# Where the weight splits of the first block stand in ScalarE's queue

## The chip, the cores and the metric

The kernel runs on one core of one Trainium2 chip. The metric is the device time of one execution in microseconds (us). Engines are called as in the profile: PE is TensorE (matmuls), ACT is ScalarE, DVE is VectorE, POOL is GpSimd, SP is SyncE, which here only issues transfers (DMA).

## The reference

One step of a hybrid recurrent decoder: 2048 prompt tokens and 64 sample tokens (8 sequences of 8), 1024 channels. What is computed, shortened:

```python
u = rms_norm(x, norm_pre)
z = u @ w_in        # lru_x, lru_gate, q|k|v, gdn_gate, b, a, two merge gates
lru_xc = conv4(lru_x) + lru_conv_b
h = rg_lru(lru_xc, ...)              # gates by 8 blocks of 128, then a scan over time
lru_out = h * silu(lru_gate)
qkv = silu(conv4(gdn_qkv))           # 8 heads of 128
gdn_out = norm(gated_delta_rule(l2norm(q), l2norm(k), v, g, beta)) * silu(gdn_gate)
merged = sigmoid(m_lru) * (lru_out @ w_br_lru) + sigmoid(m_gdn) * (gdn_out @ w_br_gdn)
y = x + rms_norm(merged @ w_out, norm_post)
```

All is in float32. States of the convolutions, of the LRU and of the delta rule are outputs too.

## The kernel before

**Precision.** A float32 product is made of three matmuls of rounded parts: every operand is held as a high part and the rest. For weights, `split` writes `hi` (ScalarE, a rounding copy) and then `lo` = source - `hi` (GpSimd; VectorE for `w_out`). A projection accumulates hi x high (L551), hi x rest (L553) and lo x high (L555) for each of eight k steps, so the third matmul of a projection is the first that needs `lo`. In the trace both parts of a weight have the name `whl`; the raw weight is `raw`, `raws` or `rawo` (128 x 1024).

**Blocks.** The prompt is done in four blocks of 512 tokens. The first block also takes the 64 sample tokens (576 columns, in halves of 256 and 320). In the first block each of 88 weight tiles is loaded, split, used, and stored to a scratch place in DRAM (`dW`, by SP); the later blocks read it back prepared. A ring of three `whl` buffers holds the split weights, so a split waits until the store of the buffer's last content has ended.

**Order of the first block.** First `u` is normalised and transposed: `u_norm` and eight `u_tile`s, each with ScalarE writing the high part `a` of 512 and of 64 columns and VectorE the rest (L358). A small projection with 16 columns of `w_in` (for beta and the decay; its weights are cast from `wraw` to `wst3`) follows. Then the *K stage*: for heads 0 to 7 the projection K (evacuated by ScalarE into `cvr`, `cvy`, `cvs`, then the convolution on VectorE, L582 for the prompt and L588 for the samples, then `th`, a tanh on ScalarE) and a merge-gate projection M (evacuated into `tmo`, which is stored as `dtm`). Then the *LRU stage*: eight groups X of 128 channels, with M8 to M14 between them; the convolved group is split into `xh` and `xl`, the block gates' weights `gwr` into `gwh` and `gwl`, and the gate matmuls (`g`) are evacuated by ScalarE into `lt`. Then the *Q stage*: per head Q, V and the head's gate, with the delta rule of the heads woven in, then the two branch projections, and `w_out` in four column groups of two weights each (evacuated with `yj`).

**What sets the order.** TensorE's order is the order of the program text. On the other engines a scheduler orders instructions by their priority, as dependences allow. `wfetch` is what brings weights: it issues the load of a raw weight, the store of an older split one, and the split. In the first block `proj` takes the next weight and calls `wfetch(1)`, so the split of weight n+1 stands in the text at the start of projection n. `A`, which stands for ScalarE, is a wrapper: when `A.after` is set, each later ScalarE instruction of the text gets an edge (of order, without a semaphore) behind that instruction:

```python
            if self.after is not None:
                self._tc.add_manual_dep(r.ins, self.after.ins.name, ..., reason="weights first")
```

`proj` sets `A.after` to the newest split. The scheduler can thus place a split early, ahead of older ScalarE work, and nothing younger may pass it.

Of the kernel before, what the change touches and what calls it, by code (L numbers as in the profile page):

```python
# [154 lines left out]
def body(ctx, tc, x_prompt, x_sample, state_lru_conv, state_lru_h, state_gdn_conv, state_gdn_S,  # L155
# [5 lines left out]
    V, T, SP = nc.vector, nc.tensor, nc.sync  # L161
    A, G = Ordered(tc, nc.scalar), nc.gpsimd
# [32 lines left out]
    def tr(out, in_, idn):  # L195
        T.transpose(out, in_, idn)  # L196
        W.pe(TR)
# [5 lines left out]
    def split(hi, lo, src, eng=None):  # L203
        r = A.activation(hi, src, AF.Copy)
        (eng or G).tensor_tensor(out=lo, in0=src, in1=hi.bitcast(F32), op=OP.subtract)  # L205
        return r
# [28 lines left out]
    key = lambda e: (e[0].tensor.name, e[1])  # L235
# [4 lines left out]
    wstores, wraws = [], {}  # L240

    wready = []
    wlast = [None]
    wnext, lnext = [0], [0]
    ring, wx = [0], []

    def wtile():
        ring[0] += 1
        if wx and ring[0] % 4 == 0:
            return wx[0].tile([128, 2, 1024], F32R, name="whx", tag="whx")  # L250
        return wp.tile([128, 2, 1024], F32R, name="whl", tag="whl", bufs=3)

    def wload(n):

        src, c = e = worder[n]
        if key(e) in wraws:
            return
        if isinstance(c, tuple):
            raw = rw.tile([128, 4, 256], F32, name="rawo", tag="raws")
            SP.dma_start(raw, src[c[1] * 512:(c[1] + 1) * 512, c[0] * 256:(c[0] + 1) * 256]  # L260
                         .rearrange("(k p) c -> p k c", p=128))
            wraws[key(e)] = raw
        elif not (paired[0] <= n < paired[1] or paired[2] <= n < paired[3]):
            raw = rw.tile([128, 8, 128], F32, name="raws", tag="raws")
            SP.dma_start(raw, src[:, c:c + 128].rearrange("(k p) c -> p k c", p=128))
            wraws[key(e)] = raw
        else:
            two = [key(x) for x in worder[n:n + 7]].count((src.tensor.name, c + 128))
            w = 128 + 128 * two
            raw = rp[0].tile([128, 8, w], F32, name="raw", tag="raw")  # L270
            SP.dma_start(raw, src[:, c:c + w].rearrange("(k p) c -> p k c", p=128))
            for j in range(1 + two):
                wraws[src.tensor.name, c + 128 * j] = raw[:, :, 128 * j:128 * j + 128]

    def wstore(held=0):

        while len(wstores) > held:
            i, hl = wstores.pop(0)
            SP.dma_start(dW[i], hl.bitcast(F32))

    def wfetch(ahead):

        while wnext[0] < len(worder) and len(wready) < ahead:
            n = wnext[0]
            e = worder[n]
            place = wplace[key(e)]
            out = isinstance(e[1], tuple)
            hl = wtile()
            hi, lo = (hl[:, j].rearrange("p (k c) -> p k c", c=256 if out else 128) for j in range(2))
            if n < len(wplace):  # L290
                while lnext[0] < len(wplace) and lnext[0] <= n + (
                        2 if paired[0] <= lnext[0] < paired[1] else 1):
                    wload(lnext[0])
                    lnext[0] += 1
                wstore(1)
                wlast[0] = split(hi, lo, wraws[key(e)], V if out else None)
                wstores.append((place, hl))
            else:
                wstore()
                SP.dma_start(hl.bitcast(F32), dW[place])  # L300
            wready.append((hi, lo))
            wnext[0] += 1
# [21 lines left out]
    def u_load(bn, pool):  # L324
        nt = NCH + (1 if bn == SB else 0)
        xh = []
        for i in range(nt):
            m = 128 if i < NCH else NS
            xt = pool.tile([128, D], F32, name=f"ux{i}")
            SP.dma_start(xt[:m], xp[bn * TB + i * 128: bn * TB + (i + 1) * 128] if i < NCH else xs)  # L330
            xh.append((xt, m))
        return xh
# [44 lines left out]
    wst3 = wst[:, 0:256].rearrange("p (k c) -> p k c", c=32)  # L377
# [34 lines left out]
    with tc.tile_pool(name="init", bufs=2, side="right") as ip:  # L412
        with tc.tile_pool(name="u0", bufs=1) as up:
            r0 = ip.tile([8, 128], F32, name="r0")
            SP.dma_start(r0, rows(norm_pre))
            xh = u_load(0, up)
            t = gtile()
            tr(t[:, :8], r0, ident[:8, :8])
            V.tensor_copy(npre, t[:, :8])
            wraw = ip.tile([128, 8, 16], F32, name="wraw", bufs=1)  # L420
            SP.dma_start(wraw, win[:, C_B:C_B + 16].rearrange("(k p) c -> p k c", p=128))
            u_norm(xh, up)
            for n in range(2):
                wload(n)
                lnext[0] += 1
            SP.dma_start(dtb, bass.AP(tensor=gdn_dt_bias.tensor, offset=gdn_dt_bias.offset, ap=[[0, 128], [1, 8]]))
            SP.dma_start(negA, bass.AP(tensor=gdn_A_log.tensor, offset=gdn_A_log.offset, ap=[[0, 128], [1, 8]]))
            u = [u_tile(xh, k) for k in range(8)]
            zz = ip.tile([128, 96], F32, name="zz", bufs=1)
            V.memset(zz, 0.0)  # L430
            V.tensor_copy(wst[:, 256:352], zz)
            V.tensor_copy(wst3[:, :, 0:16], wraw)
            V.tensor_tensor(out=wst3[:, :, 16:32], in0=wraw, in1=wst3[:, :, 0:16].bitcast(F32), op=OP.subtract)
            wfetch(2)
        G.affine_select(out=tri, in_=ones, pattern=[[1, 128]], compare_op=OP.is_ge, fill=0.0,
                        base=0, channel_multiplier=-1)
        G.affine_select(out=offm.rearrange("p (a b) -> p a b", b=32), in_=ones.rearrange("p (a b) -> p a b", b=32),
                        pattern=[[-32, 4], [0, 32]], compare_op=OP.is_ge, fill=0.0, base=-32,
                        channel_multiplier=1)
        V.tensor_scalar(offm, offm, -1.0, None, op0=OP.mult)  # L440

        blk = const.tile([64, 64], F32, name="blk")
        blk3 = blk.rearrange("p (a b) -> p a b", b=8)
        G.affine_select(out=blk3, in_=ones[:64, :64].rearrange("p (a b) -> p a b", b=8),
                        pattern=[[-8, 8], [0, 8]], compare_op=OP.is_ge, fill=0.0, base=0, channel_multiplier=1)
        G.affine_select(out=blk3, in_=blk3, pattern=[[8, 8], [0, 8]], compare_op=OP.is_ge, fill=0.0,
                        base=7, channel_multiplier=-1)
        tris = const.tile([64, 64], F32, name="tris")
        V.tensor_tensor(out=tris, in0=blk, in1=tri[:64, :64], op=OP.mult)
        negs = const.tile([64, 64], F32, name="negs")  # L450
        V.tensor_scalar(negs, tris, 1.0, BIG, op0=OP.subtract, op1=OP.mult)
        bsel = blk3[:, :, 0]
        G.memset(halog, 0.0)
        G.memset(halol, 0.0)
        G.memset(hlast, 0.0)
        tc.keep_in_program_order(A.activation(negA, negA, AF.Exp))
        V.tensor_scalar(negA, negA, -1.0, None, op0=OP.mult)
# [73 lines left out]
    for blkno in range(NBLK):  # L531
# [9 lines left out]
        def proj(mov, evac):  # L541
            w = nextw()
            wfetch(3 if blkno else 1)
            A.after = wlast[0]
            hi, lo = w
            for c0, n in halves:
                ps = pmm.tile([128, 512], F32, name="mm", tag="mm")
                for k in range(8):
                    mh, ml = mov[k]
                    wh = hi[:, k, :]  # L550
                    T.matmul(ps[:, :n], wh, mh[:, c0:c0 + n], start=k == 0, stop=False)  # L551
                    W.pump(n * 0.4219)
                    T.matmul(ps[:, :n], wh, ml[:, c0:c0 + n], start=False, stop=False)  # L553
                    W.pump(n * 0.4219)
                    T.matmul(ps[:, :n], lo[:, k, :], mh[:, c0:c0 + n], start=False, stop=k == 7)  # L555
                    if k < 7:
                        W.pump(n * 0.4219)
                evac(ps, c0, n)
                W.pump(n * 0.4219)
# [654 lines left out]
        for k in range(8):  # L1214
            hi = pA.tile([128, TB + NS], F32R, name="a", tag="a")
            lo = pA.tile([128, TB + NS], F32R, name="a", tag="a")
# [20 lines left out]
        for dd in range(8):  # L1237
# [5 lines left out]
            hi = Bp.tile([128, NB], F32R, name="bt", tag="bt")  # L1243
            lo = Bp.tile([128, NB], F32R, name="bt", tag="bt")
# [108 lines left out]
```

## Time and profile before

| | |
|---|---|
| time, median of 3 runs | 2684.38 us (2678.17 to 2687.7) |
| profiled execution, its own time | 2683.59 us |
| its span | 2681.9 us |
| mean granted TensorE clock | 0.987 |
| PE busy | 2571.7 us (96%) |
| DVE, ACT, POOL busy | 1503.4, 885.4, 565.8 us (56%, 33%, 21%) |

The span is the time from the first to the last instruction of the profiled execution; a share is of the span. A row of the timeline has the start, the duration, engine, line, operation, and the tiles with the shape; in brackets is the engine's idle time before the instruction and what released it. L143 is the line in the wrapper at which each ScalarE instruction is made, so ScalarE's work is told apart by its tiles. The first block ends at about 868 us of the span.

### The profile page before, as it was taken

Reading aid. Unit: us, or ns where it says so; the run is one execution under the profiler, and the core shown is the slowest. Engines: PE = TensorE matmul, PEld = TensorE weight load, DVE = VectorE, ACT = ScalarE, POOL = GpSimd, SP = SyncE. Lnnn points to the kernel's source line nnn. Section 1 sums busy time; section 2 is a strip of 40 time slices with the busy share of each in tenths; the row PEclk is TensorE's granted clock in tenths of the full one; section 3 lists DMA queues with packets and bytes.
Section 4 is the critical chain, followed back from the end, with each engine's and each line's share of the span. In section 5 each row is a group of like instructions: output and inputs, shape, how many; then the busy total and the mean of one; then the engine's idle time right before and its main releaser. Section 6 shows DMA issues by size and latency. Waiting matters only on the chain.

```text
span 2681.9 us, 39950 instructions
## 1 busy us (share of the span) xinstructions
PE 2571.7 (96%) x15332; PEld 2237.5 (83%) x15332; DVE 1503.4 (56%) x3441; ACT 885.4 (33%) x1722; POOL 565.8 (21%) x444
## 2 busy tenths in 40 slices
PE   6888799999999999999999999999999999999999
PEld 5887798888999788888889888888889888888888
DVE  4668477787434557566522557566513458566512
ACT  5324543333324225333302235333303235333301
POOL 2442342232540211100120121110210211110200
PEclk9988899999999999999999999999999999999999
DMA  7987978789887887554466787544466887555465
GB/s 190 250 257 187 228 207 187 203 176 179 255 292 256 283 277 222 200 177 158 154 237 256 260 283 225 203 163 163 154 245 256 270 272 217 200 172 168 160 236 200
DMA packets 327897, 581.82 MB, mean 217 GB/s; under 512 B 70849, under 2 KB 236762, under 8 KB 282650
## 3 DMA queue, kind: packets, MB, share of 16 engines
q1 hardware_dynamic: 313882, 553.57, 66.9%
q10 hardware_dynamic: 13824, 25.70, 2.5%
q8 instruction: 121, 1.98, 0.3%
q14 instruction: 70, 0.57, 0.1%
HBM read 421.61 MB, written 157.59 MB: 216 GB/s over the span
## 4 chain that ended last, share of the span: by engine, by line
PE 68%; DMA 3%; issue 2%; DVE 1%; POOL 1%; ACT 1%; SPq 0%; ACTq 0%; POOLq 0%; DVEq 0%
PE mm L555 17%; PE mm L551 16%; PE mm L553 16%; PE g L192 5%; PE c L192 4%; PE mm L1294 2%; PE mm L1298 2%; PE mm L1296 2%; PE g L196 2%; DMA er<-dgc 1%; DMA dgc<-gr 0%; DMA npb<-in_norm_post_dram 0%; DMA ux<-in_x_prompt_dram 0%; DMA whl<-dW 0%; POOL er L756 0%
## 5 line engine op out<-in xcount | busy, mean ns | idle before, releaser
L551 PE MATMUL mm<-a,whl 128*128 128x512 f32 (+2 forms) x2432 | 865.0, 356 | 25.2 <-ACT tmo L143 18.5
L555 PE MATMUL mm<-a,whl 128*128 128x512 f32 (+2 forms) x2432 | 869.6, 358 | 4.8 <-POOL whl L205 4.8
L553 PE MATMUL mm<-a,whl 128*128 128x512 f32 (+2 forms) x2432 | 863.9, 355 | 0.0
L551 PEld LDWEIGHTS mm<-a,whl 128*128 128x128 f32 x2432 | 466.7, 192 | 74.7 <-ACT tmo L143 20.0
L555 PEld LDWEIGHTS mm<-a,whl 128*128 128x128 f32 x2432 | 466.7, 192 | 58.0 <-POOL whl L205 5.4
L553 PEld LDWEIGHTS mm<-a,whl 128*128 128x128 f32 x2432 | 466.7, 192 | 45.6
L582 DVE SCALAR_TENSOR_TENSOR cvy<-cvr,cwg,cvy 128x512 f32<-128x512 f32 x288 | 224.7, 780 | 17.8 <-ACT cvy L143 12.4
L553 PE MATMUL mm<-a,whx 128*128 128x512 f32 x448 | 181.7, 406 | 0.0
L555 PE MATMUL mm<-a,whx 128*128 128x512 f32 x448 | 181.4, 405 | 0.0
L551 PE MATMUL mm<-a,whx 128*128 128x512 f32 x448 | 179.3, 400 | 0.0
L1232 DVE SCALAR_TENSOR_TENSOR pt<-tm,mm 128x512 f32<-128x512 f32 (+1 forms) x80 | 47.4, 592 | 189.8 <-PE mm L555 189.8
L143 ACT ACTIVATE cvr<-mm 128x512 f32<-128x512 f32 (+1 forms) x160 | 81.7, 510 | 175.4 <-PE mm L555 167.3
L1086 POOL TENSOR_TENSOR st<-st,mhalf 128x4 f32<-128x4 f32 x32 | 32.3, 1009 | 507.8 <-DVE st L1084 496.0
L205 POOL TENSOR_TENSOR whl<-raw,whl 128x1024 fp32r<-128x1024 f32 x44 | 108.8, 2474 | 118.4 <-ACT whl L143 108.6
L205 POOL TENSOR_TENSOR whl<-raws,whl 128x1024 fp32r<-128x1024 f32 x36 | 89.8, 2495 | 188.6 <-ACT whl L143 176.5
L1296 PE MATMUL mm<-whl,bt 128*128 128x256 f32 x448 | 126.4, 282 | 0.8 <-DVE whl L205 0.8
L1294 PE MATMUL mm<-whl,bt 128*128 128x256 f32 x448 | 126.2, 282 | 0.8 <-DVE y L1303 0.8
L1298 PE MATMUL mm<-whl,bt 128*128 128x256 f32 x448 | 126.2, 282 | 0.6 <-DVE yss L1272 0.6
L143 ACT ACTIVATE th<-cvy 128x512 f32<-128x512 f32 (+1 forms) x96 | 61.9, 644 | 195.7 <-DVE cvy L582 128.6
L143 ACT ACTIVATE yv<-c 128x128 f32<-128x128 f32 x128 | 35.5, 278 | 243.7 <-PE c L192 243.2
L555 PE MATMUL mm<-gp,whl 128*128 128x512 f32 (+2 forms) x296 | 104.2, 352 | 0.0
L551 PE MATMUL mm<-gp,whl 128*128 128x512 f32 (+2 forms) x296 | 104.1, 352 | 0.0
(341 smaller groups left out, 4637.8 us busy)
## 6 DMA issues: line engine op xcount, KB each, us to landing
whl<-dW SPq DMA_DIRECT2D x199, 1024.0 KB
dW<-whl SPq DMA_DIRECT2D x88, 1024.0 KB
whx<-dW SPq DMA_DIRECT2D x65, 1024.0 KB
raws<-in_w_in_dram SPq DMA_DIRECT2D x33, 512.0 KB
raw<-in_w_in_dram SPq DMA_DIRECT2D x15, 1024.0 KB
dtm<-tmo ACTq DMA_DIRECT2D x48, 256.0 KB
tm<-dtm SPq DMA_DIRECT2D x48, 256.0 KB
ux<-in_x_prompt_dram SPq DMA_DIRECT2D x16, 512.0 KB
```

Source lines behind the costliest of these rows:

```text
L143: r = f(*args, **kw)
L192: T.matmul(out, a, b, start=start, stop=stop)
L196: T.transpose(out, in_, idn)
L205: (eng or G).tensor_tensor(out=lo, in0=src, in1=hi.bitcast(F32), op=OP.subtract)
L551: T.matmul(ps[:, :n], wh, mh[:, c0:c0 + n], start=k == 0, stop=False)
L553: T.matmul(ps[:, :n], wh, ml[:, c0:c0 + n], start=False, stop=False)
L555: T.matmul(ps[:, :n], lo[:, k, :], mh[:, c0:c0 + n], start=False, stop=k == 7)
L582: V.scalar_tensor_tensor(out=y[:, :TB], in0=raw[:, i:i + TB], scalar=cw[:, i, ti:ti + 1], in1=y[:, :TB], op0=OP.mult, op1=OP.add)
L1232: proj(mov, lambda ps, c0, n: V.scalar_tensor_tensor(out=t_[:, c0:c0 + n], in0=x[:, c0:c0 + n], scalar=1.0, in1=ps[:, :n], op0=OP.add, op1 ...
L1294: T.matmul(ps[:, :256], mh[:, cs], wh[:, k % 4], start=k == 0, stop=False)
L1296: T.matmul(ps[:, :256], mh[:, cs], wl[:, k % 4], start=False, stop=False)
L1298: T.matmul(ps[:, :256], ml[:, cs], wh[:, k % 4], start=False, stop=k == 7)
```

## The change

The wrapper's edge is never set any more. Instead each split is pinned behind the ScalarE instruction that stands just before it in the text (`keep_in_program_order`: the instruction may not come before the one that its engine was given last). The memset of `zz` and the cast of beta's weights are pinned in the same way behind VectorE's last instruction in the text, which is of the `u` tiles.

```diff
@@ -240,7 +240,6 @@
     wready = []
-    wlast = [None]
     wnext, lnext = [0], [0]
@@ -293,7 +292,7 @@
                 wstore(1)
-                wlast[0] = split(hi, lo, wraws[key(e)], V if out else None)
+                tc.keep_in_program_order(split(hi, lo, wraws[key(e)], V if out else None))
                 wstores.append((place, hl))
@@ -427,9 +426,9 @@
             u = [u_tile(xh, k) for k in range(8)]
             zz = ip.tile([128, 96], F32, name="zz", bufs=1)
-            V.memset(zz, 0.0)
+            tc.keep_in_program_order(V.memset(zz, 0.0))
             V.tensor_copy(wst[:, 256:352], zz)
-            V.tensor_copy(wst3[:, :, 0:16], wraw)
+            tc.keep_in_program_order(V.tensor_copy(wst3[:, :, 0:16], wraw))
             V.tensor_tensor(out=wst3[:, :, 16:32], in0=wraw, in1=wst3[:, :, 0:16].bitcast(F32), op=OP.subtract)
             wfetch(2)
@@ -541,7 +540,6 @@
             w = nextw()
             wfetch(3 if blkno else 1)
-            A.after = wlast[0]
             hi, lo = w
```

What this does to ScalarE's order, at three places. At the start, before, from the first split on (`a` is the high part of a `u` tile, `ux` the scaled input):

```order
L143 ACTIVATE ux_216<-ux_216,urr 128x1024
L143 ACTIVATE whl<-raws 128x1024
L143 ACTIVATE a<-g,npre 128x512
L143 ACTIVATE a<-g,npre 128x64
L143 ACTIVATE a<-g,npre 128x512
L143 ACTIVATE whl<-raws 128x1024
```

And now, from the last `u` tile on:

```order
L143 ACTIVATE a<-g,npre 128x512
L143 ACTIVATE a<-g,npre 128x64
L143 ACTIVATE whl<-raws 128x1024 x2
L143 ACTIVATE negA<-negA 128x8
L143 ACTIVATE zr<-mm 32x256
L143 ACTIVATE zr<-mm 32x320
```

All sixteen writes of `a` now come ahead of the two first splits, and the third split has gone from among them into the K stage.

In the K stage, at the end of the second K projection, before (`whl` is the next K weight, `th` the tanh of the head, `tmo` the evacuation of the merge-gate projection that TensorE does meanwhile):

```order
L143 ACTIVATE cvs<-mm 128x8x8
L143 ACTIVATE whl<-raw 128x1024
L143 ACTIVATE th<-cvy 128x576
L143 ACTIVATE tmo<-mm 128x256
L143 ACTIVATE tmo<-mm 128x320
```

And now:

```order
L143 ACTIVATE cvs<-mm 128x8x8
L143 ACTIVATE th<-cvy 128x576
L143 ACTIVATE whl<-raw 128x1024
L143 ACTIVATE tmo<-mm 128x256
L143 ACTIVATE tmo<-mm 128x320
```

The split of the next K weight has gone from before to behind the tanh. It is the same at the other heads, and in the Q stage with the tanh of V and the next Q weight.

In the LRU stage, at the sixth group, before, with the numbers of the tiles (`whl_3129` is M13's weight, `whl_3231` the next group's):

```order
L143 ACTIVATE gwh_3120<-gwr_3117 128x256
L143 DMA dtm_197<-tmo_3025 128x576
L143 ACTIVATE whl_3129<-raw_2736 128x1024
L143 ACTIVATE cvr_3124<-mm_3135 128x256
L143 ACTIVATE cvy_3125<-mm_3135,par_178 128x256
L143 ACTIVATE whl_3231<-raw_3027 128x1024
L143 ACTIVATE lt_3180<-g_3181,hba_187 128x256
L143 ACTIVATE lt_3180<-g_3186,hba_187 128x320
L143 ACTIVATE la_3204<-lt_3180,ls4_188 128x576
```

And now, from the evacuation of that group's second half on:

```order
L143 ACTIVATE cvr_3124<-mm_3162 128x256
L143 ACTIVATE cvy_3125<-mm_3162,par_178 128x320
L143 ACTIVATE cvs_3127<-mm_3162 128x8x8
L143 ACTIVATE xh_3237<-cvy_3125 128x576
L143 ACTIVATE gwh_3120<-gwr_3117 128x256
L143 ACTIVATE whl_3129<-raw_2736 128x1024
L143 ACTIVATE whl_3231<-raw_3027 128x1024
L143 ACTIVATE tmo_3230<-mm_3235 128x256
```

Both splits have gone from before the `lt` evacuations to behind the group's `xh` and the gates' `gwh`.

## Rows read from the trace of the kernel before

**Rows 1.** Busy time by engine of the K stage: stretch, its us, PE, PEld, DVE, ACT, POOL (instructions), clock, DMA share, GB/s.

```profile
44.60:183.00 138.40, 121.13 (x858) 117.08 (x858) 83.96 (x243) 48.60 (x107) 57.48 (x41) 0.95 0.92 270
```

**Rows 2.** Waits of PE, K and LRU stages (44.6 to 331.2): total, times, longest us.

```profile
PE mm L551 <- ACT tmo L143: 18.5, 6, 7.3
PE g L192 <- ACT lt L143: 15.1, 2, 10.1
PE mm L555 <- POOL whl L205: 4.8, 2, 2.9
...
PE mm L551 <- ACT cvy L143: 2.7, 1, 2.7
```

**Rows 3.** Waits of ACT in the same stretch.

```profile
ACT whl L143 <- DMA dW<-whl: 47.4, 10, 8.8
ACT er L143 <- POOL er L757: 31.7, 7, 9.7
```

**Rows 4.** Timeline of the start (ACT, DVE and PE).

```profile
14.57 1.15 ACT L143 ACTIVATE ux<-ux,urr 128x1024 f32<-128x1024 f32 x1 [1.84 <-POOL urr L341]
...
31.44 1.06 ACT L143 ACTIVATE whl<-raws 128x1024 fp32r<-128x1024 f32 x1 [5.51 <-DMA raws<-in_w_in_dram]
32.41 1.45 ACT L143 ACTIVATE a<-g,npre 128x512 fp32r<-128x512 f32 x3
...
37.42 0.94 DVE L358 SCALAR_TENSOR_TENSOR a<-g,npre,a 128x512 fp32r<-128x512 f32 x2 [0.40 <-ACT a L143]
...
44.62 0.39 PE L551 MATMUL mm<-a,whl 128*128 128x256 f32 x1
```

**Rows 5.** The page's groups: busy us, mean ns, idle before and releaser.

```profile
L205 POOL TENSOR_TENSOR whl<-raw,whl 128x1024 fp32r<-128x1024 f32 x44 | 108.8, 2474 | 118.4 <-ACT whl L143 108.6
```

**Rows 6.** Timeline of head 1 of the K stage, by engine.

```profile
66.26 0.28 PE L551 MATMUL mm<-a,whl 128*128 128x256 f32 x1
...
72.65 0.28 PE L551 MATMUL mm<-a,whl 128*128 128x256 f32 x1
...
67.25 1.07 ACT L143 ACTIVATE whl<-raw 128x1024 fp32r<-128x1024 f32 x1
...
72.21 0.69 ACT L143 ACTIVATE th<-cvy 128x576 f32<-128x576 f32 x1 [3.89 <-DVE cvy L588]
...
68.40 2.78 POOL L205 TENSOR_TENSOR whl<-raw,whl 128x1024 fp32r<-128x1024 f32 x1 [4.38 <-ACT whl L143]
...
67.96 0.28 DVE L588 SCALAR_TENSOR_TENSOR cvy<-cvs,cwg,cvy 128x64 f32<-128x64 f32 x1
68.82 2.44 DVE L588 SCALAR_TENSOR_TENSOR cvy<-cvs,cwg,cvy 128x64 f32<-128x64 f32 x1
```

**Rows 7.** Timeline of the LRU stage, fifth and sixth group.

```profile
281.47 0.41 PE L551 MATMUL mm<-a,whl 128*128 128x256 f32 x1
...
306.57 0.63 PE L192 MATMUL g<-xh,gwh 128*128 128x320 f32 x1 [10.10 <-ACT lt L143]
...
288.14 0.69 ACT L143 ACTIVATE xh<-cvy 128x576 fp32r<-128x576 f32 x1 [1.42 <-DVE cvy L588]
...
305.10 1.06 ACT L143 ACTIVATE whl<-raw 128x1024 fp32r<-128x1024 f32 x1 [6.97 <-issue]
```

**Rows 8.** Timeline of the Q stage, from V of head 3 to Q of head 4.

```profile
510.25 2.43 DVE L588 SCALAR_TENSOR_TENSOR cvy<-cvs,cwg,cvy 128x64 f32<-128x64 f32 x1
...
514.08 0.28 PE L551 MATMUL mm<-a,whl 128*128 128x256 f32 x1
...
517.01 0.65 PE L196 MATMUL g<-ident,cvy 128*128 128x128 f32 x4 [1.35 <-DVE cvy L597]
...
514.50 0.69 ACT L143 ACTIVATE th<-cvy 128x576 f32<-128x576 f32 x1 [3.98 <-DVE st L1084]
```

**Rows 9.** Timeline of w_out, second column group.

```profile
850.80 1.22 DVE L205 TENSOR_TENSOR whl<-rawo,whl 128x1024 fp32r<-128x1024 f32 x1 [1.53 <-ACT whl L143]
...
851.80 1.06 ACT L143 ACTIVATE whl<-rawo 128x1024 fp32r<-128x1024 f32 x1
```

## The prediction

> **What bounds the kernel now.** I read the stages first, by busy time. In the stretch of the eight K heads of the first block [rows 1] TensorE is busy for 121.13 of 138.40 us, so 17.3 us are lost there, and the sixteen DMA engines are at a share of 0.92 with 270 GB/s: transfers are nearly full. The later blocks read prepared weights, and their instruction order is the same before and after the change on each engine; I take their time as unchanged. So all that can move lies in the first block, and the question is which wait of TensorE ends last there.
>
> The waits of TensorE over the K and LRU stages [rows 2] name ScalarE's results: six waits of 18.5 us for `tmo` (the release of a projection's PSUM buffer; the longest is 7.3), two of 15.1 for `lt` (an LRU gate's evacuation, 10.1 the longest), one of 2.7 for `cvy`, and two of 4.8 for the GpSimd half of a split. Then what ScalarE itself waited for [rows 3]: its split waits 47.4 us, in ten pieces, until the store of the buffer's old content to DRAM has ended. As `A.after` ties every later ScalarE instruction of the text behind the split, an evacuation that TensorE needs stands behind that wait. The second row of the same group is another matter: `er` waits 31.7 us for GpSimd, and the 7.3 us wait for `tmo` stands behind one of those (9.7 us). The change doesn't remove it, as `er` keeps its place among the evacuations.
>
> **The change, part by part.** All sums are against the profiled execution's own 2683.59 us, which is 0.8 below the median of the three runs.
>
> *Start.* Now a split stands between the writes of the `u` tiles, and ScalarE waits for weights while tiles could be written: 5.51 us in the one row shown [rows 4]. After the change all sixteen writes come first. The last three-row group of writes starts at 32.41 with five tiles to go, and the last VectorE half ends at 37.42 + 0.94 = 38.36: 1.19 us a tile. The scaled input is there at 14.57 + 1.15 = 15.72. Eight tiles at that pace from then end at about 25 to 26, some 12 us sooner than now. The first K projection starts at 44.62, 6.3 us behind the last tile. It can't take the whole 12: the splits of the first two weights now follow the tiles (two of 1.06 and a GpSimd half), and the parameter loads and third weight come in their own time. I take -9 (-7 to -11). The beta casts and the memset behind VectorE's tile writes lie in this term: they feed the small projection that runs when the tiles are complete, and are worth less than a microsecond each if they are last.
>
> *Waits that go.* With older work ahead of the split, an evacuation no longer stands behind a wait for a store. Of rows 2 that is 18.5 - 7.3 = 11.2, 15.1, 4.8 and 2.7, together 33.8. I take -29, since a split still sits ahead of some evacuations (the merge-gate weight's is followed by the next head's). Bounds: -15 (the stores stay late, and half comes back as a wait for the split itself) to -34.
>
> *New waits in the K stage.* The split of the next K weight now stands behind `th`, the tanh of the current K head, and that waits for VectorE's convolution. K1 ends at 66.26 and M1 runs until 72.65 [rows 6], so K2's weight has 6.39 us, and its third matmul needs the GpSimd half 0.2 later. `th` starts at 72.21. One convolution step of 64 columns takes 0.28 us at 67.96 but 2.44 at 68.82, and that one ends at 71.26, just after the GpSimd half of a split (68.40, 2.78 long). If that split has gone behind `th`, the stretch of 2.16 goes, and `th` starts at 70.05, which is 3.8 after K1's end. Then `th` 0.69, ScalarE's half 1.06 to 1.07, GpSimd's 2.47 by its mean [rows 5]: ready at 3.8 + 0.7 + 1.06 + 2.47 = 8.0, needed at 6.6, a wait of 1.4. With the stretch left in place it is 3.6. I take 2 at each of eight heads: +16 (11 to 29).
>
> The Trainium skill ("SBUF — State Buffer", section "SBUF: two separate sides") says that VectorE and GpSimd share a port pair that is locked for a whole instruction, and that a VectorE operation with two SBUF inputs blocks until a GpSimd operation that reads SBUF has ended. The 2.44 beside 0.28 agrees with it. By that rule the stretch doesn't vanish: the GpSimd half now runs later, against the product of `th` and `cvy` or the L2 work, and each head would pay the 2.16 at its other end. That is the second rival below.
>
> *New waits in the LRU stage.* In the sixth LRU group the split of M13's weight now stands behind the group's own evacuations, `xh` and `gwh` (order shown above). In the group before, `xh` starts at 288.14 [rows 7], 6.7 after the projection's end at 281.47. From there 0.69 for it, some 0.4 for `gwh`, 1.06 for the split and 2.4 for the GpSimd half: 11.2 after the end of the projection. TensorE has a few gate matmuls in between, and part of the 6.7 is other VectorE work that comes earlier if 10 us less is lost at 306.57, so I take 8. M10's split has also moved behind a `gwh`, about 3. Together +11 (3 to 15). On the other side the split at 305.10, which had waited 6.97 us, no longer holds `lt`; that is the 10.10 of the matmul at 306.57, already in the waits that go.
>
> *Q stage.* In seven heads the split of the next Q weight goes from before to behind the tanh of V. For head 4, Q starts at 514.08 and the tanh at 514.50 [rows 8]. The stretched step (2.43 at 510.25) would go, so the tanh at about 512.35, then 0.69, 1.06 and 2.47: ready at 516.6 where 514.3 is wanted, 2.3 late. But TensorE waits 1.35 at 517.01 for what follows that tanh, and that wait would end inside the new one. Net about 1 each: +6 (0 if there is as much slack as the shift, 17 at 2.4 each).
>
> *The w_out stage.* The second weight's split of each of the three later column groups goes behind the last evacuation of the group before: it starts at 851.80 where the earlier one started two microseconds before [rows 9]; 1.06 + 1.22 later its halves are there, at 854.1, and the fifth k step wants them at about 852.9. That is 1.2 each, +4 (0 to 5). Branch weights: the split moves behind a `bt` write and its half is ready just when the next branch projection starts, so 0; if not, 8 times some tenths.
>
> Sum: -9 - 29 + 16 + 11 + 6 + 4 = -1, or 2682.6; with the 0.8 to the median, **2683**.
>
> **The rivals.** 0.3% is about what a measurement of this kernel can tell from no change: 8 us, so 2676.3 and 2692.4.
>
> *Faster.* The new waits are small since each earlier evacuation makes the split earlier too. For it: 47.4 us of ScalarE's waiting is for stores, and a split that stands later waits less. Start -11, waits -34, K 8 x 1.4 = +11, LRU +3, Q and w_out 0: -31, so 2653. Against it: the tanh is late by VectorE's own work.
>
> *Slower.* GpSimd's half still stretches a VectorE step, now behind the tanh: K 8 x 3.6 = +29, LRU +15, Q +17, w_out +4, against -9 and -29: +27, so 2711. It decides from 0.7 us extra at each of the fifteen places on (10 us together). For it: the stretch is seen in both stages [rows 6, 8]. Against it: a late wait absorbs what follows it.
>
> *Transfers pace the K stage.* At a share of 0.92 [rows 1] the K waits that go come back as waits for raw weights, and the new ones lie under them: 16.0 isn't gained and 16 not paid. Start -9, LRU -17.8 + 11, Q and w_out +10: -6, so 2678. Against it: none of the listed waits of TensorE is for a transfer.
>
> **How the numbers follow.** Forecast (no measurable change; its own range 2673 to 2693) 0.38, faster rival 0.30, slower rival 0.22, transfers 0.10. Range: 2650 takes in the faster rival nearly whole; 2706 leaves out the far end of the slower one, whose half is 2697. Faster by over 0.3%: 0.30, with 0.10 from the low ends of the forecast and of the transfers; slower: most of its rival and the forecast's upper end, 0.25; same 0.35.
>
> **What would show it.** Right: the first K projection at 34 to 37 instead of 44.62; ScalarE's wait of 47.4 for stores much smaller; no `lt` wait of 10; new waits of TensorE for the GpSimd half at K heads (1.4 to 3.6) and M13; no 2.4 us convolution step ahead of `th`. Wrong: if waits for the split at each K and Q head are nil (faster) or over 3 (slower), or if the stages end when they did in spite of a start that is 9 us sooner.

## The result and the profile after

The changed kernel takes 2720.89 us (median of 4 runs, 2719.78 to 2724.56) where the one before took 2683.2 (4 runs): a ratio of 1.0143, 95% interval 1.0122 to 1.0164. It is 1.4% slower; the forecast was no change, and the time lies above the range. The profiled execution of the changed kernel took 2719.78 us with a span of 2718.1, so the two spans differ by 36.2 us, and this is the sum to be explained.

In the changed kernel the three matmuls of a projection have the lines L549, L551 and L553 (hi x high, hi x rest, lo x high), the samples' convolution has L586, and the three matmuls of `w_out` have L1292, L1294 and L1296.

A table of stages comes first, read from the timeline of TensorE: a stage starts with the first matmul of its first weight. Each number is the stage's length after the change less its length before.

| stage (starts in before, us) | after - before, us | forecast |
|---|---|---|
| up to the first K projection (0 to 44.62) | -7.0 | -9 |
| K (to 183.04) | +16.7 | K and LRU together: -29 + 16 + 11 = -2 |
| LRU groups (to 339.24) | -11.4 | |
| first gates (to 366.43) | +0.7 | 0 |
| Q (to 683.40) | +15.2 | +6 |
| last gates (to 713.96) | 0.0 | 0 |
| branches (to 816.00) | +7.7 | 0 |
| w_out (to 879.41) | +9.0 | +4 |
| the rest, three blocks (to 2681.9) | +5.3 | 0 |

The last row starts with the second block's first matmul, so for TensorE the first block of the kernel before ends at 879.41, not at the 868 that was given for it above.

The waits of TensorE in the K and LRU stages of the changed kernel answer to [rows 2] (total us, times, longest):

```profile
PE mm L549 <- ACT whl L143: 30.5, 7, 9.6
PE mm L553 <- POOL whl L205: 21.0, 13, 3.6
PE g L192 <- ACT xh L143: 3.1, 1, 3.1
PE g L192 <- DVE xl L205: 0.8, 1, 0.8
PE g L192 <- ACT lt L143: 0.3, 1, 0.3
```

The waits for `tmo`, `lt` and `cvy` have gone but for 0.3 us, as the change means: evacuations no longer stand behind splits. In their place TensorE waits for the splits themselves, 51.5 us in 20 pieces. What ScalarE waited for in the same stretch answers to [rows 3]:

```profile
ACT er L143 <- POOL er L755: 35.3, 8, 9.0
ACT whl L143 <- DMA dW<-whl: 11.7, 2, 10.9
```

The wait for stores fell from 47.4 to 11.7 us, as the splits now come later. `er` still waits for GpSimd, and GpSimd ahead of it for a transfer (`er<-dgc`, 25.9 us in the K stage, 32.6 before).

The start answers to [rows 4]: the tiles are complete at 26, as worked out, and then TensorE waits for what stands behind the pinned casts (DVE, POOL and PE; the MEMSET is `zz`, the CAST beta's weights):

```profile
25.05 0.94 DVE L357 SCALAR_TENSOR_TENSOR a<-g,npre,a 128x512 fp32r<-128x512 f32 x2 [0.54 <-ACT a L143]
25.96 0.14 DVE L429 MEMSET zz<- 128x96 f32 x1
...
26.26 0.22 DVE L431 CAST wst<-wraw 128x128 fp32r<-128x128 f32 x1
...
26.54 2.29 DVE L432 TENSOR_TENSOR wst<-wraw,wst 128x128 fp32r<-128x128 f32 x1
...
26.25 4.81 POOL L205 TENSOR_TENSOR whl<-raws,whl 128x1024 fp32r<-128x1024 f32 x2 [1.58 <-ACT whl L143]
...
28.98 6.71 PE L192 MATMUL mm<-a,wst 128*128 128x256 f32 x32 [4.23 <-DVE wst L432]
37.62 0.39 PE L549 MATMUL mm<-a,whl 128*128 128x256 f32 x1
```

Two heads of the K stage, each by engine. A plain one answers to [rows 6]: K1 ends at 63.83, the tanh comes 3.79 later (3.8 was worked out), and TensorE's wait for the GpSimd half at K2 is 1.13:

```profile
63.83 0.28 PE L549 MATMUL mm<-a,whl 128*128 128x256 f32 x1
71.76 0.38 PE L553 MATMUL mm<-a,whl 128*128 128x256 f32 x1 [1.13 <-POOL whl L205]
...
67.62 0.69 ACT L143 ACTIVATE th<-cvy 128x576 f32<-128x576 f32 x1 [2.67 <-DVE cvy L586]
68.21 1.04 ACT L143 ACTIVATE whl<-raw 128x1024 fp32r<-128x1024 f32 x1
...
69.33 2.37 POOL L205 TENSOR_TENSOR whl<-raw,whl 128x1024 fp32r<-128x1024 f32 x1 [12.67 <-ACT whl L143]
```

And the next head, where an `er` stands ahead of the tanh:

```profile
92.49 0.63 ACT L143 ACTIVATE er<-er 128x512 f32<-128x512 f32 x1 [5.24 <-POOL er L755]
93.02 0.67 ACT L143 ACTIVATE th<-cvy 128x576 f32<-128x576 f32 x1
...
93.60 1.04 ACT L143 ACTIVATE whl<-raw 128x1024 fp32r<-128x1024 f32 x1
...
90.71 1.04 POOL L754 TENSOR_TENSOR er<-er,gcs 128x512 f32<-128x512 f32 x1 [2.38 <-DMA er<-dgc]
...
96.72 4.67 POOL L205 TENSOR_TENSOR whl<-raw,whl 128x1024 fp32r<-128x1024 f32 x2
...
94.69 0.58 PE L549 MATMUL mm<-a,whl 128*128 128x256 f32 x1 [5.20 <-ACT whl L143]
99.11 0.58 PE L553 MATMUL mm<-a,whl 128*128 128x256 f32 x1 [3.62 <-POOL whl L205]
```

The split of K3's weight now inherits the wait of the `er` ahead of the tanh: 5.20 us, and 3.62 more since GpSimd was busy with the next `er` when the split's first half was ready. It recurs at K5 (5.77 + 1.63) and K7 (5.30 + 1.64).

In the Q stage, TensorE's largest waits were these before, each about once a head:

```profile
PE g L196 <- DVE cvy L597: 9.4, 7, 1.4
PE c L192 <- DVE S L1072: 6.8, 7, 1.3
```

And they are these now (`Dn` is a single wait for a transfer):

```profile
PE mm L553 <- POOL whl L205: 20.8, 10, 2.5
PE c L192 <- DVE X L1059: 8.3, 6, 1.4
PE g L192 <- DMA Dn<-dD: 4.2, 1, 4.2
```

Head 4 answers to [rows 8] (ACT and PE):

```profile
514.38 0.69 ACT L143 ACTIVATE th<-cvy 128x576 f32<-128x576 f32 x1 [2.01 <-DVE st L1082]
514.98 1.04 ACT L143 ACTIVATE whl<-raws 128x1024 fp32r<-128x1024 f32 x1
...
506.37 0.49 PE L192 MATMUL c<-X,R 128*128 128x128 f32 x2 [1.39 <-DVE X L1059]
519.11 0.58 PE L553 MATMUL mm<-a,whl 128*128 128x256 f32 x1 [2.53 <-POOL whl L205]
```

V ends at 509.71, so the tanh is 4.67 behind it, and the wait is 2.53 where 2.3 was worked out. Behind it the granted clock falls (stretches of the Q stage by busy time; the three numbers at a row's end are clock, DMA share and GB/s):

```profile
505.00:510.00 5.00, 3.63 (x30) 3.64 (x31) 3.48 (x11) 0.96 (x3) 0.74 (x1) 1.00 0.79 147
510.00:515.00 5.00, 5.00 (x40) 5.00 (x40) 4.09 (x14) 2.34 (x7) 0.56 (x1) 1.00 0.93 340
515.00:520.00 5.00, 2.47 (x15) 2.20 (x14) 2.09 (x4) 2.67 (x5) 4.36 (x3) 0.87 0.06 20
520.00:525.00 5.00, 5.00 (x35) 4.77 (x35) 2.58 (x6) 0.96 (x2) 1.72 (x2) 0.79 0.80 188
525.00:530.00 5.00, 5.00 (x46) 4.33 (x44) 4.41 (x12) 1.50 (x4) 1.08 (x1) 1.00 1.03 254
```

Where TensorE had been busy throughout, the clock is at its full level; with and after the 2.53 us wait a part of ten microseconds is granted the lower one (1.2 of 2.4 GHz). The shorter wait of 1.39 us at 506.37 left it at 1.00, and so did the one of 1.35 before:

```profile
513.00:518.00 5.00, 3.65 (x30) 3.45 (x29) 4.03 (x13) 2.23 (x4) 2.20 (x2) 1.00 0.96 168
```

The lower clock is a cost beside the wait: over the whole execution PE's busy time is 2587.0 us where it was 2571.7, for the same 15332 matmuls, so 15.3 of the 36.2 us are matmuls that ran slower, net of those that ran faster. The other 21 are idle time.

### The profile page after: what moved, and what is told of

It reads as the page before. It is cut to its first block, busy times and chain, and to the rows that moved or that the text cites. A ratio compares the mean times of both kernels' runs of the same rounds, so it can differ in the third digit from the quotient of the medians.

```text
span 2718.1 us, 39968 instructions
## 1 busy us (share of the span) xinstructions
PE 2587.0 (95%) x15332; PEld 2248.5 (83%) x15332; DVE 1460.3 (54%) x3441; ACT 886.9 (33%) x1722; POOL 559.9 (21%) x444
## 4 chain that ended last, share of the span: by engine, by line
PE 61%; DMA 4%; issue 2%; DVE 1%; POOL 1%; ACT 1%; SPq 0%; ACTq 0%; POOLq 0%; DVEq 0%
PE mm L553 15%; PE mm L551 15%; PE mm L549 15%; PE g L192 5%; PE c L192 4%; PE mm L1294 2%; PE mm L1296 2%; PE mm L1292 2%; PE g L196 2%; DMA er<-dgc 1%; DMA dE<-er 1%; DMA xr<-in_x_prompt_dram 0%; POOL er L754 0%; DMA ux<-in_x_prompt_dram 0%; DMA dgc<-gr 0%
## 5 line engine op out<-in xcount | busy, mean ns | idle before, releaser
L553 PE MATMUL mm<-a,whl 128*128 128x512 f32 (+2 forms) x2432 | 873.6, 359 | 41.8 <-POOL whl L205 41.8
L549 PE MATMUL mm<-a,whl 128*128 128x512 f32 (+2 forms) x2432 | 867.6, 357 | 31.0 <-ACT whl L143 30.5
L551 PE MATMUL mm<-a,whl 128*128 128x512 f32 (+2 forms) x2432 | 865.4, 356 | 0.0
L553 PEld LDWEIGHTS mm<-a,whl 128*128 128x128 f32 x2432 | 468.4, 193 | 99.8 <-POOL whl L205 46.9
L549 PEld LDWEIGHTS mm<-a,whl 128*128 128x128 f32 x2432 | 468.5, 193 | 81.3 <-ACT whl L143 32.3
L551 PEld LDWEIGHTS mm<-a,whl 128*128 128x128 f32 x2432 | 468.5, 193 | 45.7
L580 DVE SCALAR_TENSOR_TENSOR cvy<-cvr,cwg,cvy 128x512 f32<-128x512 f32 x288 | 217.3, 755 | 19.2 <-ACT cvy L143 13.6
L551 PE MATMUL mm<-a,whx 128*128 128x512 f32 x448 | 181.7, 406 | 0.0
L553 PE MATMUL mm<-a,whx 128*128 128x512 f32 x448 | 181.4, 405 | 0.0
L549 PE MATMUL mm<-a,whx 128*128 128x512 f32 x448 | 179.3, 400 | 0.0
L1294 PE MATMUL mm<-whl,bt 128*128 128x256 f32 x448 | 128.6, 287 | 4.8 <-DVE whl L205 4.8
L1292 PE MATMUL mm<-whl,bt 128*128 128x256 f32 x448 | 128.2, 286 | 2.7 <-ACT whl L143 2.7
L1296 PE MATMUL mm<-whl,bt 128*128 128x256 f32 x448 | 127.7, 285 | 0.0
L143 ACT ACTIVATE bt<-pt 128x512 fp32r<-128x512 f32 (+1 forms) x32 | 20.6, 644 | 279.0 <-POOL pt L1240 273.6
L553 PE MATMUL mm<-gp,whl 128*128 128x512 f32 (+2 forms) x296 | 105.6, 357 | 2.0 <-POOL whl L205 2.0
```

What stands on the lines that cost most here:

```text
L143: r = f(*args, **kw)
L580: V.scalar_tensor_tensor(out=y[:, :TB], in0=raw[:, i:i + TB], scalar=cw[:, i, ti:ti + 1], in1=y[:, :TB], op0=OP.mult, op1=OP.add)
L1292: T.matmul(ps[:, :256], mh[:, cs], wh[:, k % 4], start=k == 0, stop=False)
L1294: T.matmul(ps[:, :256], mh[:, cs], wl[:, k % 4], start=False, stop=False)
L1296: T.matmul(ps[:, :256], ml[:, cs], wh[:, k % 4], start=False, stop=k == 7)
```

## The experiments

The kernels ran on several chips, each beside the kernel before, so ratios are compared. Stage numbers are lengths less those of the profile of before, as in the table above; each is from one profiled execution. How far such a number can be trusted is seen where two executions have the same instruction order on ScalarE, VectorE and GpSimd. The run with the Q stage's splits pinned has the order of the kernel before up to the first gates, and its K stage is 3.2 us shorter; the run with free `w_out` splits has the order of the changed kernel up to the last branches, and its Q stage is 4.2 us longer. A difference of up to about 4 us in one stage is therefore no finding by itself.

**The casts alone.** Both VectorE pins in the kernel before:

```diff
-            V.memset(zz, 0.0)
+            tc.keep_in_program_order(V.memset(zz, 0.0))
...
-            V.tensor_copy(wst3[:, :, 0:16], wraw)
+            tc.keep_in_program_order(V.tensor_copy(wst3[:, :, 0:16], wraw))
```

> Only the beta casts and the memset are tied behind VectorE's input work; splits as before. Theory (the whole difference comes from where the splits stand): the first K projection starts within 2 us of 44.62 and the time is that of before, 2681 to 2687. Rival (the casts made the start 7 us shorter by giving VectorE to the tiles first): the first K projection near 38 and a time near 2676.

2671.21 beside 2678.45: 0.9972 (0.9962 to 0.9983). The first K projection is 2.4 us *later* (47.05), so the rival is wrong on the place, and the theory is wrong on the time: the LRU stage is 10.5 us shorter and the Q stage 5.4, though no split was touched. ScalarE's and GpSimd's orders differ between 77 us, in the K stage, and 320, at the end of the LRU stage: `er` and splits stand elsewhere among the evacuations. How the scheduler comes to that from two pins at the start isn't shown. In the Q stage the order is that of the kernel before, and so are the waits for `cvy` and `S`; 4.4 of its 5.4 us are a shorter busy time of TensorE, whose granted clock near the stage's start was 0.73 to 0.93 in places before and 1.00 in this run. So a stage's difference is not the price of an edit in that stage unless the stages ahead of it are the same.

**Start and LRU splits pinned, the rest as before.**

```diff
+                r = split(hi, lo, wraws[key(e)], V if out else None)
+                if n < 3 or 16 <= n < 31:
+                    tc.keep_in_program_order(r)
+                else:
+                    wlast[0] = r
```

> Splits 0 to 2 (start) and 16 to 30 (LRU stage) are pinned behind older ScalarE work; all others hold younger work behind them as before, and the casts are as before. Theory (the change gains 7 us at the start and 11 in the LRU stage and loses 17, 15, 8 and 15 in the K, Q, branch and w_out stages): 18 faster, near 2665, up to 2661 if the small projection no longer waits 4.23 us for the pinned casts. Rival (what is gained early is lost again since the transfers set when the Q stage can start): within 5 us of 2683.

2674.64 beside 2678.45: 0.9987 (0.9973 to 1.0001). That is 3.5 us faster where the theory had 18, so the time is the rival's. In the profiled execution the start gains 9.9 us (first K at 34.69, with free casts) and the LRU stage 7.4, the K stage is 4.4 longer, and the whole is 14.7 shorter; but it is one of the two fastest of ten runs, and the rival's reason, that the Q stage can't start sooner, doesn't show in it.

**The same form for the K stage alone** (`3 <= n < 16`).

> The kernel before, with the splits of the K stage alone (weights 3 to 15) pinned behind older ScalarE work. Theory (the tail of er, tanh, split and GpSimd half at the heads): K0 to X0 takes 150 to 157 us instead of 138.4, and the time is 8 to 18 above before. Rival (the loss of the changed kernel's K stage comes with its earlier start, since the same transfers then have less time): K0 to X0 within 5 us of 138.4.

2680.75 beside 2677.03: 1.0009 (0.9992 to 1.0026). The K stage is 11.0 longer (149.4 us), just below what was expected; the LRU stage is 9.9 shorter with its splits untouched, so the time stays, where 8 to 18 more were expected. With the casts' run it shows that the LRU stage's -11.4 after the change is not the pins' alone.

**The same form for the Q stage alone** (`35 <= n < 59`).

> The kernel before, with the splits of the Q stage alone (weights 35 to 58) pinned behind older ScalarE work. Theory (in that stage each Q weight's split behind the tanh of V is late by itself): a head's period goes from 38.3 us to 40 to 41.6, the stage is 12 to 17 us longer, and the time is 10 to 18 above before. Rival (the Q stage was slow in the changed kernel since all of its stages were shifted and the scheduler set another order): the period stays within 0.5 us of 38.3 and the time within 4 of before.

2699.8 beside 2677.03: 1.0070 (1.0042 to 1.0097). By the ratio that is 19 us, just over the theory's 10 to 18. Up to the first gates it has the order of the kernel before (K -3.2, LRU +0.1), then Q is 13.9 longer, and nothing after it is given back. TensorE's waits in that stage (L559 is the third matmul):

```profile
PE mm L559 <- POOL whl L205: 17.7, 8, 2.5
PE c L192 <- DVE X L1065: 10.4, 6, 3.5
```

The theory holds: the pins of this stage by themselves make its loss, and the waits are again for the GpSimd half and for `X`. The three splits of a head weren't pinned one by one; that it is the Q weight's, behind the tanh of V, is read from the rows of head 4.

**`er` out of the way in the changed kernel.** In the first block the exponential is put behind the tanh of the next head:

```diff
+            t0 = W.t
+            if not blkno:
+                yield lambda: thd[0] > h + 1 or thd[0] == H
             act(er, er, AF.Exp)
             A.dma_start(dE[h], er.rearrange("p c i -> p (c i)"))
-            yield T_GRAM
+            yield max(0.0, T_GRAM - (W.t - t0))
```

`thd[0]` counts the heads whose tanh is in the program.

> The changed kernel, with the exponentials of the Gram factors (er) of the first block put into the program behind the tanh of the next K head, so that they stand behind the next K split on ScalarE. Theory (in the K stage the split is late since the tanh ahead of it stands behind an er that waits up to 9 us for GpSimd): the waits for ScalarE's half at K3, K5 and K7 (5.2, 5.8, 5.3) go and the ones for GpSimd's half shrink to 0.7, so 16 to 22 faster than the changed kernel, near 2702. Rival (the tanh is late by VectorE's convolution and the port that it shares with GpSimd): at most 4 us.

1.0138 (1.0097 to 1.0179), from three runs of 2704.27 to 2722.54: no gain is shown, and the time alone decides little. Yet the mechanism shows: TensorE's waits in the K stage, first of the changed kernel, then of this one:

```profile
PE mm L549 <- ACT whl L143: 16.9, 4, 5.8
PE mm L553 <- POOL whl L205: 13.3, 8, 3.6
```

```profile
PE mm L553 <- POOL whl L205: 17.9, 8, 3.8
PE mm L549 <- ACT whl L143: 3.2, 2, 2.6
```

The waits for ScalarE's half fell by 13.7 us and the stage by 6.7 (+10.1 in place of +16.7), but waits for GpSimd's half rose by 4.6. The LRU stage is 4.7 longer than in the changed kernel, and the later blocks 5.5. `er` is a part of the K loss; the expected 16 to 22 was not there.

**Splits half a projection ahead.** The weight after next is split between the halves of a projection:

```diff
+                if not blkno and not c0:
+                    wfetch(2)
                 evac(ps, c0, n)
```

> The changed kernel, with the split of the weight after next put into the program between the two halves of each projection of the first block, so that it is pinned behind the first half's predecessor instead of the tanh. Theory (all new waits are the tail tanh, split, GpSimd half): the waits at K heads, Q heads and branches go, the gains at the start and in the LRU stage stay: 20 to 45 faster than the changed kernel, 2675 to 2700. Rival (an earlier split finds its buffer not stored or its raw weight not there, and ScalarE's evacuations wait behind it as before): between 2700 and 2721, with ScalarE's waits for stores back above 30 us.

2678.45 beside 2678.45: 0.9997 (0.9983 to 1.0011), some 39 us below the changed kernel by the ratios. Start and LRU keep -7.1 and -9.0, K is +0.9, Q -5.4, branches 0.0; `w_out` keeps its +8.3, and the later blocks are at +7.0. The rival's sign isn't there: ScalarE's splits wait 20.2 us for stores over the K and LRU stages, not over 30.

**w_out's splits free, in the changed kernel** (`if not out:` ahead of the pin).

> The changed kernel, with the eight splits of w_out neither pinned nor holding others: the scheduler may place them. Theory (the second weight of a column group is late behind the last evacuation of the group before, and the start of the second block loses 5.7 us after the slower w_out stage): w_out takes 63 to 64 us as before instead of 72.4, the second block's start is back, and the time is 9 to 15 below the changed kernel. Rival (w_out is slow since the next block's input work shares its engines): at most 3 us below the changed kernel.

1.0083 (1.0054 to 1.0111), by the ratios some 16 us below the changed kernel, a little over the theory. `w_out` is back at -0.5. The profiled execution (2711.58) lies above the median of 2700.77, so its other stages are not compared, and whether the second block's start is back can't be told from it (later blocks +3.5).

**Branch and w_out splits free** (`if n < 64:`).

> The changed kernel with the splits of the branch weights and of w_out free. Theory (the branch stage's 7.7 us and w_out's 9.0 come from the pins there): branch stage 102.1 as before instead of 109.7, w_out 63 instead of 72.4, and the time 16 to 24 below the changed kernel. Rival (the first branch projection is late since the Q stage ends later and the raw branch weights and LRU halves come later with it): the branch stage stays above 106.

1.0098 (1.0080 to 1.0116), by the ratios 12 us below the changed kernel, less than was expected. In the profiled execution everything ahead is as in the changed kernel (K +17.0, LRU -10.7, Q +15.2), and behind it the branch stage is at 0.0, `w_out` at 0.0 and the later blocks at -1.1: by stages the pins there cost 7.7 + 9.0 + 6.4, about 23 us, and the profiled times differ by 22 (2697.9 against 2719.78). That execution is the fastest of its four, though, the others being 2701.76 to 2703.45. So the place is shown, and the price is 12 to 23 us; beside the run with only `w_out` free the times show no further gain.

**The changed kernel with free casts.**

> The changed kernel without the two pins on VectorE (the memset and the beta casts are free). Theory (the 4.23 us for which TensorE waits for the pinned casts are a loss at the start alone): the small projection starts at 27 instead of 28.98, the first K projection at 35 to 36 instead of 37.62, and the time is 1 to 4 below the changed kernel. Rival (any shift at the start lets the scheduler set another order of the K and LRU stages, as the casts alone did in the kernel before): K and LRU stages together change by more than 5 us in either direction.

1.0152 (1.0135 to 1.0169), within the changed kernel's interval. The small projection starts at 27.00 as expected, the first K projection at 34.37, 3.25 sooner, and K and LRU together are at +4.4 in place of +5.4: the theory's place and, at the start, more than its size. The time, expected 1 to 4 lower, shows nothing of it.

**Toward a faster kernel.** Splits ahead, w_out free, casts free:

> The changed kernel with three edits together: the split of the weight after next stands between the halves of a projection, w_out's splits are free, and the beta casts are not pinned. Theory (what is lost in the K, Q and branch stages is the tail of tanh, split and GpSimd half; what is lost in w_out is its pin; 4.2 us at the start are the pinned casts): the gains add up, 12 to 24 below before, with the first K projection at 34 to 35. Rival (each shift at the start makes the scheduler set another order in the K and LRU stages, and those swing by 10 us either way): between 8 below and 6 above before.

2664.59 beside 2677.03: 0.9944 (0.9924 to 0.9965), the low end of the theory's range, with the first K projection at 35.71. The same with pinned casts:

> The kernel with splits half a projection ahead and free w_out splits, but with the beta casts pinned. Theory (pinned casts cost 2 us at the start and nothing else): 8 to 12 below before. Rival (the pinned casts change the order of the K and LRU stages for the better, as alone in the kernel before): 16 or more below before.

2661.28 beside 2676.91: 0.9949 (0.9932 to 0.9966), 14 to 16 us below, between theory and rival, and the same as with free casts within the intervals. And the first with `er` late:

> The kernel with splits half a projection ahead, free w_out splits and free casts, and in addition er behind the tanh of the next head in the first block. Theory (er's wait for GpSimd still stands ahead of splits and tanhs in the K stage, where single weights take 13 to 18 us): the K stage is 4 to 12 us shorter, 16 to 28 below before. Rival (the K stage is now paced by transfers at a share of 0.94 and more): within 3 us of the same kernel without this edit, 10 to 16 below before.

1.0003 (0.9990 to 1.0017): K is 5.1 longer than before instead of 0.3 shorter, so moving `er` is a loss here. Neither the theory nor the rival names why, but the two profiles show where: in the K stage ScalarE's splits wait 30.1 us for stores, where they waited 9.7 without this edit, and TensorE waits 10.0 for `tmo` in place of 4.9. In the run with pinned casts TensorE's Q waits are these, over all eight heads:

```profile
PE c L192 <- DVE S L1074: 5.9, 7, 0.9
PE g L196 <- DVE cvy L599: 5.5, 7, 0.8
```

The wait for a Q weight is gone from the list, and the wait for `cvy` that stood in [rows 8] at 1.35 is at most 0.8. Both kernels with splits ahead and a free w_out beat both the kernel before and the changed one.

## Why the prediction was wrong

**Start: right mechanism, 2 us off.** -7.0 in place of -9, and the first K projection at 37.62, just outside the 34 to 37 that was named. The tiles end at 26 as worked out. The casts were priced at less than a microsecond each, and TensorE waits 4.23 us for them: behind the tiles, `wst`'s subtraction meets the first splits' GpSimd half and takes 2.29 us, where the same operation took 0.27 in the run with the casts alone. This is the port rule that the prediction took from the Trainium skill ("SBUF — State Buffer", "SBUF: two separate sides"), and it agrees here. With the casts free the start is 10.2 shorter, inside the -7 to -11 that was given.

**The stretch at the tanh: right.** No `L586` step of a K or Q head is longer than 0.28 us, and the two tails (3.79 and 4.67 behind the projection) are as worked out. The slower rival came nearest in time (2711), by luck, with a mechanism that did not happen: the GpSimd half does not stretch a step behind the tanh that anyone waits for.

**"I take 2 at each of eight heads": the step that failed in the K stage.** Behind heads without an `er` ahead of the tanh the wait was small: 2.5 at K1, 1.13 at K2, 0.71 at K4, 0.70 at K6 and at the first LRU group. K3, K5 and K7 waited 8.8, 7.4 and 6.9, so it was 28.9 in all where 16 was taken. The prediction had named `er`'s wait of 31.7 us and its place among the evacuations, took it as unchanged, and did not see that the tanh, and with it the split, would queue behind it. Before, the split stood ahead of the tanh. The `er` run shows the link (16.9 to 3.2 us of waits), if no gain in time, and the K stage's run shows that the pins of that stage alone make it 11.0 longer.

**The LRU stage: near, by two errors.** M13's wait is 9.64 + 1.63 where 8 was taken, and the new waits for splits come to 20.6 where 11 was; the `lt` wait of 10.10 is gone. TensorE idled 49.0 us in the K and LRU stages before and 56.1 now, 51.5 of it for splits where 27 was taken; so all but 4.6 of the old waits went, where 29 were to go. Even the 7.3 us for `tmo` went, which the prediction left standing: the K3 projection, in which it fell, now waits for its split instead, behind an `er` too. The two sums are each out by 15 or more and offset each other, which is luck. And two runs with untouched LRU splits gained 10 us there as well, so the LRU stage proves little.

**Q stage: mis-sized, +15.2 for +6.** The wait itself is right (2.53 for 2.3). "Net about 1 each" failed: the waits for `cvy` (9.4) and `S` (6.8) went, but 20.8 came for the split, 8.3 for `X` in six heads and 2.8 more for `Dn`; with some 4 us of single waits gone, TensorE idles 11.1 us longer in the stage. The other 4.0 are matmuls that ran slower, which the sum left out; the rows of head 4 show the lower clock behind the 2.53 us wait. That the total is near the far end (17 at 2.4 each) is luck: that end had no clock in it.

**Branches and w_out: mis-sized.** "Ready just when the next branch projection starts, so 0" holds for the later branches. The second GDN branch projection (`gp` in the rows) is what failed: its split is pinned behind the last high part of the LRU output, which waits for GpSimd. ACT and PE there, with the clock of that stretch:

```profile
733.98 0.69 ACT L143 ACTIVATE a<-lru 128x576 fp32r<-128x576 f32 x1 [3.99 <-POOL lru L937]
734.57 1.99 ACT L143 ACTIVATE whl<-raws 128x1024 fp32r<-128x1024 f32 x2
...
735.66 0.39 PE L549 MATMUL mm<-gp,whl 128*128 128x256 f32 x1 [0.93 <-ACT whl L143]
738.20 0.58 PE L553 MATMUL mm<-gp,whl 128*128 128x256 f32 x1 [2.03 <-POOL whl L205]
...
735.00:740.00 5.00, 2.31 (x10) 2.10 (x11) 1.67 (x3) 2.28 (x3) 4.63 (x3) 0.71 1.05 322
740.00:747.00 7.00, 7.00 (x41) 7.00 (x40) 0.42 (x1) 0.33 (x1) 2.85 (x2) 0.72 1.03 408
```

The two waits are 3.0 of the stage's 7.7 us, and a wait of 1.4 for the first `w_out` weight falls into the stage as well; the other 3.3 are matmuls that took longer, at the clock of 0.71 and 0.72. In `w_out` the three later groups waited 3.4 us in all, where +4 was taken; the first group, which the prediction did not look at, waited 4.1 (that 1.4 included; 2.2 before), its splits standing on ScalarE behind the next block's input work. The larger part of `w_out`'s +9.0, 5.1 us, is again the clock: 0.72 in the 18 us from 838, where the first 18 us of the stage had 1.00 before.

**Later blocks: "I take their time as unchanged" failed by 5.3.** Their order is unchanged, but the second block starts behind a different end of the first: TensorE waits 2.96 us for `zr`, and the clock is 0.90 in the first 35 us of that block where it was 1.00 (2.6 us are idle time, 2.7 slower matmuls). With the branch and w_out pins gone it is back.

So the sum missed 37 us, in about this order: Q 9, branches 8, K and LRU 7, w_out 5, later blocks 5, start 2 and the first gates 1. What was common to most of them: a pin behind "the instruction traced just before" inherits everything that instruction waits for, and the longer of the resulting waits cost clock as well. For the clock the prediction has no term at all, and it is 15.3 of the 36.2 us.

**Open:** how the scheduler comes to the order that made the LRU stage 10 us shorter in the casts' run and in the K run, and why `er` behind the tanh brings the K splits against the stores in one kernel and not in the other.

## What to carry to other kernels

Before a split or a prefetch is tied behind older work, read what the instruction just ahead of it waits for in the trace, and what stands ahead of that: the tail from there to the last engine has to fit before the weight is needed. If it doesn't, move the split's place in the program rather than its tie; half a projection sooner was worth about 39 us here. Look at the first item of each stage by itself, since the steady part hid two of the losses, and judge an edit by a run in which all that is ahead of it stays the same.

## What the runs showed of the hardware

A wait can cost TensorE more than its length: in the stretches of 5 to 7 us with and behind the waits of 2.0 and 2.5 us shown above the granted clock was 0.71 to 0.87, and PE's busy time grew by 15.3 us for the same matmuls. With the single waits of 1.35 and 1.39 us it was 1.00. And a VectorE subtraction of 0.27 us became one of 2.29 beside a GpSimd subtraction.
